# A hybrid layer's kernel: GDN's pools at the right end of memory, attention's first steps beside GDN's last pair, and another tile for two of RWKV's inverses

## The chip, the cores and the metric

The kernel runs on one core of one Trainium2 chip. The metric is the device time of one execution in microseconds (us). TensorE is PE in the rows, its weight loads are PEld, VectorE is DVE, ScalarE is ACT, GpSimd is POOL and SyncE, which here issues DMAs, is SP.

## The reference, cut to what matters

All is float32; 1024 positions (T) of width 1024. Two layers of `first_block` are followed by one `second_block`, which the change doesn't touch.

```python
for layer in range(2):
    h = rms_norm(x, norm_g[layer])
    cols = split_columns(h @ w_in[layer])       # 27 tiles of 128 columns
    y_gdn  = gdn_branch(cols, ...)              # 6 heads, conv of 5, chunks of 64, both directions
    y_mla  = mla_branch(cols, positions, ...)   # 6 heads of softmax attention over 1024 keys
    y_rwkv = rwkv7_branch(cols, ...)            # 4 heads, both directions
    mix = concatenate([y_gdn, y_mla, y_rwkv]) * silu(cols['gate'])
    x = x + mix @ w_out[layer]

# gdn_branch, in a chunk and then over the chunks:
sol = triangular_solve(a_mat, rhs, unit_diagonal=True)      # needs the inverse of a 64x64 triangle
u = u0_c - w_c @ s;  o = qg_c @ s + p_c @ u;  s = ge_c * s + kd_c.T @ u
# mla_branch:
q = rms_norm(cq) @ w_uq;  k, v = rms_norm(ckv) @ w_ukv;  rope on 32 of 96 columns
o = softmax(q @ k.T * scale) @ v
# rwkv7_branch: a token shift, decays and keys, then a scan of the same kind as GDN's
```

The three branches need only `cols`. GDN and RWKV each have a serial scan over chunks; attention has none.

## The kernel before, in words

`layer` (L1658 on) computes one of the two layers in two phases and then the out-projection.

**Phase 1** is the projection beside GDN. The normalised input lies split in two parts, `hh` and `hl`, in pool h. `dense_steps` yields the 1296 products of the 27 tiles one at a time (48 each, `product` L1045, into `psd`), with weights loaded by SP into `wr` and split by ACT and POOL into `wh` and `wl`; ACT evicts `psd` into `st` and sends it to `proj` in DRAM. `paced` ties the products to a count that SP waits on, so that the loads keep step. GDN has three pairs of heads. `gdn_front` is a generator of five stages for one pair: convolution, products, the inverse of the lanes on DVE (`lane_inverse` with `lan`), then on PE L358 to L371 (the inverse's larger blocks), L382, L395 and L405. `gdn_scan` walks over the chunks: L440 writes `psk`, DVE L442 subtracts it, and the output products L428 and L430 go to `pso`; after the last step the norm of the outputs ends with DVE L458.

The string `SEQ_A` is the order of phase 1 as the program is written: a digit is the next stage of that pair, `T6` is six tiles of the projection, `S1` is the scan of pair 1. What is left of the projection, six tiles, is written after `S2`. The scheduler takes this order as priority, not as the final one: it moves an instruction ahead where a tile is free, and the final order of each engine is fixed when the kernel is built.

**Phase 2** is RWKV with attention as its filler. `SEQ_B` lists RWKV's parts: F features, V values, E early, L late, S scan, O output, for the two head groups and the two directions (0 and 1 are one group, 2 and 3 the other; odd ones are the backward direction, `d` = 1). `weave` takes eight steps of `mla` for each round of RWKV's parts, so that attention's 1146 steps are spread over them. `mla` begins with loads by POOL (`mc`, `cq`, `ckv`, L864 to L867), the norms of `cq` and `ckv` (ACT L879, PE L882, ACT L135 and L136), queries (PE L947, L948), rope (DVE and POOL L847 to L850), scores (L974), softmax (L975, L979), the transposes of the probabilities (PE L927 into `ps` of the PSUM pool mT, ACT `ph` L929, DVE `pl` L930) and values (L937 into `pso`).

`rwkv_early` (E) ends with `lan` (DVE L635) and `lane_inverse` on POOL: ACT L468 copies `lan` into `xl`, then 60 POOL instructions (L475, L476) make the inverse in place. `rwkv_late` (L) reads `xl` on DVE (L690) and PE (L698, L705). `lan`, `xl` and `lt` have one buffer each. So the copy for E1 waits until L0 has read `xl`, and that for E3 until L2 has.

Memory: phase 1 opens PSUM as pss 1 bank (the scan's own), pso 1, ps 3, psd 2, and pools h, w, g in SBUF one behind the other from the left. Phase 2 opens after all of these are closed: mT 2 banks, mS 2, rx 3, mo 1, and pools r and s (RWKV) and m (attention), again from the left. So r lies where h was, and RWKV's loads wait until the projection has read h for the last time; m lies further right, where GDN's tiles were.

Of the kernel before, what the change touches and what calls it, by code (L numbers as in the profile page):

```python
# [13 lines left out]
F32 = mybir.dt.float32  # L14
F32R = mybir.dt.float32r
I32 = mybir.dt.int32
AF = mybir.ActivationFunctionType
# [8 lines left out]
SEQ_A = "0 T6 0 1 1 T6 1 0 S0 1 1 2 2 2 T5 S1 2 2 S2"  # L26
# [69 lines left out]
class K:  # L96
# [19 lines left out]
    def psum(self, ex, **banks):  # L116

        return [
            ex.enter_context(self.tc.tile_pool(name=self.name(nm), bufs=b, space=PSUM, reuse_waits="tile"))
            for nm, b in banks.items()  # L120
        ]

    def name(self, s):
        self.n += 1
        return f"{s}_{self.n}"

# [284 lines left out]
def gdn_scan(k, hp, F, prm, y_out):  # L411
# [23 lines left out]
    for s in range(1, NST - 1):  # L435
        psk = k.pss.tile([128, 512], F32, tag="sc", name=n("psk"))
# [12 lines left out]
    for x, sl in zip(y, HALVES):  # L449
        sq = F["free"][1][:, sl]  # L450
        nc.scalar.activation(sq, x, AF.Square)
        ps = k.pss.tile([128, 512], F32, tag="sc", name=n("ps"))
# [9 lines left out]
def lane_inverse(k, eng, pool, lan):  # L462
# [3 lines left out]
    xt = pool.tile([128, 32, 32], F32, tag="xl", name=k.name("xl"))  # L466
# [80 lines left out]
def rwkv_early(k, gi, d, F, prm, P, w2a2, E):  # L547
# [91 lines left out]
    E.update(kb=kb, rk=rk, ga=ga, gb=gb, ep=ep, xl=lane_inverse(k, nc.gpsimd, g, lan))  # L639
# [442 lines left out]
def run(steps):  # L1082
    for _ in steps:
        pass
# [579 lines left out]
def layer(k, L, xs, x_in, x_out, prm_d, prm_at, w_in, w_out, wuq, wukv, cs, next_g):  # L1664
# [3 lines left out]
    with ExitStack() as lx:  # L1668
# [11 lines left out]
        with ExitStack() as hx:  # L1680
            k.pss, k.pso, k.ps, k.psd = k.psum(hx, pss=1, pso=1, ps=3, psd=2)
            hp_ = hx.enter_context(tc.tile_pool(name=n("h"), bufs=1, reuse_waits="tile"))
            hh = hp_.tile([128, 8, T], F32R, name=n("hh"))
            hl = hp_.tile([128, 8, T], F32R, name=n("hl"))
            xs.split_norm(pf("ng"), lambda i, sl: (hh[:, i, sl], hl[:, i, sl]))
            xs.close()
            with ExitStack() as gx:
                wpool = gx.enter_context(tc.tile_pool(name=n("w"), bufs=1, reuse_waits="tile"))
                k.wp = Tagged(wpool, dict(wr=2, wh=3, wl=3, st=2))

                def job(i):
                    def evac(hf, sl, ps):
                        st = k.wp.tile([128, 512], F32, tag="st", name=n("st"))[:, : sl.stop - sl.start]
                        nc.scalar.activation(st, ps, AF.Silu if i >= TI["gate"] else AF.Copy)
                        nc.scalar.dma_start(proj[i][:, sl], st)
                    return w_in[i], ((lambda j: hh[:, j]), (lambda j: hl[:, j])), evac

                steps = dense_steps(k, map(job, ORDER), wait=True)
# [156 lines left out]
```

## Time and profile before

| | us |
|---|---|
| three runs, median (lowest to highest) | 3957.01 (3955.95 to 3962.45) |
| the profiled execution, its own time | 3981.41 |
| its span in the trace | 3979.6 |
| PE busy | 3454.4 (87%) |
| DVE busy | 2349.3 (59%) |
| ACT busy | 1780.1 (45%) |
| POOL busy | 1409.3 (35%) |

In the first layer the projection and GDN run from about 40 to 637 us of the span, RWKV and attention from 637 to 1195, the out-projection to about 1310; the second layer is the same some 1280 us later, and the second block runs from about 2570 to the end. Times below are of the first layer. "Granted clock" (PEclk) is the share of full speed that TensorE was given in a stretch.

### The profile page before, as it was taken

To read this page: it belongs to the slowest core of one execution; us is meant where nothing else is said; L and a number is where in the kernel's file an instruction comes from. 1 tells how busy PE (TensorE), PEld (TensorE's weight loads), DVE (VectorE), ACT (ScalarE), POOL (GpSimd) and SP (SyncE) were. 2 spreads that over 40 slices of the span, in tenths; PEclk is the share of its full clock that TensorE was granted. 3 is DMA by queue.
4 is the path that set the end of the run, shared out by engine and by line. 5 is a ranking of instruction groups with operands and counts; after the bars stand their busy time and mean duration, and the time that the engine had idled before them with its cause. 6 is when DMAs were issued, how large, how long until landed. Compare 5 with 4: busy or idle time off the path is not lost. (4 is left out here: it accounts for less than half of the span.)

```text
span 3979.6 us, 72088 instructions
## 1 busy us (share of the span) xinstructions
PE 3454.4 (87%) x30444; PEld 2710.6 (68%) x30444; DVE 2349.3 (59%) x3138; ACT 1780.1 (45%) x2798; POOL 1409.3 (35%) x1389
## 2 busy tenths in 40 slices
PE   5897996797887889899679899779999998999898
PEld 4666673575665666667357576668888877887786
DVE  6675544857653567462575864359998975323223
ACT  5533425454552553343545454344344347555222
POOL 3431311534403343131163440433333545333361
PEclk9998997898998899899779888879999999999899
DMA  3321211000014232121100000411111111111432
GB/s 115 102 67 47 70 55 66 20 7 4 7 53 166 83 98 68 44 84 49 56 19 7 4 7 33 155 65 46 49 54 51 39 56 46 55 56 41 162 110 72
DMA packets 107076, 237.35 MB, mean 60 GB/s; under 512 B 13896, under 2 KB 16328, under 8 KB 106752
## 3 DMA queue, kind: packets, MB, share of 16 engines
q1 hardware_dynamic: 88448, 197.87, 15.3%
q10 hardware_dynamic: 17280, 31.46, 2.1%
q8 instruction: 239, 3.92, 0.4%
q0 software_dynamic: 1024, 3.41, 0.3%
q14 instruction: 85, 0.70, 0.1%
HBM read 164.17 MB, written 62.23 MB: 57 GB/s over the span
## 5 line engine op out<-in xcount | busy, mean ns | idle before, releaser
L1045 PE MATMUL psd<-hh,wh 128*128 128x512 f32 (+2 forms) x2272 | 910.3, 401 | 56.4 <-ACT hh L1002 18.9
L1006 POOL TENSOR_TENSOR wl<-wr,wh 128x512 fp32r<-128x512 f32 x332 | 489.3, 1475 | 1233.2 <-ACT wh L1002 1193.3
L1045 PE MATMUL psd<-hl,wh 128*128 128x512 f32 (+2 forms) x2272 | 864.9, 381 | 26.7 <-DVE hl L1006 21.6
L1045 PE MATMUL psd<-hh,wl 128*128 128x512 f32 (+2 forms) x2272 | 863.8, 380 | 9.3 <-POOL wl L1006 9.3
L1045 PEld LDWEIGHTS psd<-hh,wh 128*128 128x128 f32 x2272 | 441.4, 194 | 148.4 <-ACT hh L1002 22.9
L1045 PEld LDWEIGHTS psd<-hl,wh 128*128 128x128 f32 x2272 | 440.7, 194 | 100.2 <-DVE hl L1006 27.8
L1045 PEld LDWEIGHTS psd<-hh,wl 128*128 128x128 f32 x2272 | 441.3, 194 | 79.9 <-POOL wl L1006 13.1
L1002 ACT ACTIVATE wh<-wr 128x512 fp32r<-128x512 f32 x332 | 208.3, 628 | 574.4 <-PE psd L1045 345.2
L1211 DVE SCALAR_TENSOR_TENSOR co<-pad,cw,co 128x1024 f32<-128x1024 f32 x240 | 368.7, 1536 | 5.8
L929 ACT ACTIVATE ph<-ps 128x512 fp32r<-128x512 f32 x192 | 114.3, 595 | 198.3 <-PE pso L937 191.0
L930 DVE TENSOR_TENSOR pl<-ps,ph 128x512 fp32r<-128x512 f32 x192 | 131.8, 686 | 91.2 <-ACT ph L929 88.5
L975 DVE TENSOR_REDUCE m<-pss 128x1 f32<-128x512 f32 x192 | 130.6, 687 | 80.2 <-PE pss L974 78.6
L1045 PE MATMUL psd<-hi,wh 128*128 128x512 f32 x384 | 149.7, 393 | 11.7 <-ACT wh L1002 11.7
L937 PE MATMUL pso<-pl,v 128*64 128x256 f32 x384 | 111.4, 324 | 51.9 <-DVE pl L930 51.3
L937 PE MATMUL pso<-ph,v 128*128 128x256 f32 x384 | 134.3, 353 | 23.9 <-DVE y L941 17.4
L1045 PE MATMUL psd<-hi,wl 128*128 128x512 f32 x384 | 149.4, 392 | 5.3 <-POOL wl L1006 5.3
L476 POOL TENSOR_TENSOR xl<-xl,lt 64x30 f32<-64x30 f32 (+14 forms) x240 | 146.3, 609 | 18.1
L1045 PE MATMUL psd<-lo,wh 128*128 128x512 f32 x384 | 149.9, 393 | 0.0
L979 ACT ACTIVATE p<-pss,m 128x512 f32<-128x512 f32 x192 | 129.8, 683 | 44.1 <-DVE m L976 38.5
L1045 PE MATMUL psd<-mh,wh 128*128 128x512 f32 x256 | 102.1, 414 | 48.8 <-ACT wh L1002 35.9
L475 POOL TENSOR_TENSOR lt<-lan,xl 64x30 f32<-64x30 f32 (+14 forms) x240 | 134.1, 559 | 17.9
L927 PE MATMUL ps<-cst,p 128*128 128x128 f32 x768 | 137.8, 302 | 1.1 <-ACT p L979 1.1
(486 smaller groups left out, 7415.2 us busy)
## 6 DMA issues: line engine op xcount, KB each, us to landing
wr<-in_w_in SPq DMA_DIRECT2D x252, 256.0 KB, 2.7
proj<-st ACTq DMA_DIRECT2D x108, 256.0 KB, 2.1
pad<-proj SPq DMA_DIRECT2D x32, 512.0 KB, 3.7
wr<-in_w_out SPq DMA_DIRECT2D x48, 256.0 KB, 2.9
y<-yd SPq DMA_DIRECT2D x16, 512.0 KB, 5.4
sg<-proj SPq DMA_DIRECT2D x16, 512.0 KB, 4.4
x<-x SPq DMA_DIRECT2D x16, 512.0 KB, 4.1
eg<-eg SPq DMA_DIRECT2D x24, 256.0 KB, 4.1
```

Of the source, the lines that this page charges most:

```text
L475: eng.tensor_tensor(t, a, b, op=ALU.mult)
L476: eng.tensor_tensor(x[:, j + 1 :, 0:j], x[:, j + 1 :, 0:j], t, op=ALU.subtract)
L927: yield nc.tensor.transpose(ps[:, c : c + 128], p[i][kt // 4][:, (kt % 4) * 128 : (kt % 4) * 128 + 128], k.c("ident"))
L929: nc.scalar.activation(ph, ps, AF.Copy)
L930: nc.vector.tensor_tensor(pl, ps, ph.bitcast(F32), op=ALU.subtract)
L937: yield nc.tensor.matmul(o, lhsT=l, rhs=r[:, c], start=kt + i == 0, stop=kt + i == 8)
L975: nc.vector.reduce_max(m[:, h : h + 1], pss[h], axis=AX.X)
L979: nc.scalar.activation(p[h], pss[h], AF.Exp, bias=m[:, 2:3], scale=SCALE, accum_out=sums[:, t, h : h + 1])
L1002: first = nc.scalar.activation(hi, src, AF.Copy)
L1006: e.tensor_tensor(lo, src, hi.bitcast(F32), op=ALU.subtract)
L1045: yield nc.tensor.matmul(ps, lhsT=w(a)(i), rhs=x[b](i)[:, sl], start=i == 0 and a == b, stop=i == 7 and a == 1)
L1211: eng.scalar_tensor_tensor(out, pad[:, j : j + T], w[:, j : j + 1], out, op0=ALU.mult, op1=ALU.add)
```

## The change

1. **Pools.** GDN's pool g and RWKV's r and s go to the right end of SBUF; h and w, and then m of attention, lie on the left. In PSUM `pss` is gone: `psk` and the scan's norm take one of the three banks that the front also uses (`k.ps`). `psd` lies left, `pso` and `ps` right. When the projection ends, `psd` and pool h/w close and attention's mS (2 banks), mT (1) and mo (1) open in their place, while GDN still runs. The second bank of mT is opened only with phase 2, on the right; `InTurn` then alternates.
2. **Order.** `SEQ_A` has all remaining eleven tiles ahead of `S1`, and `M60`, `M150` and `M250`, 460 steps of attention, around pair 2's last stages and its scan. `attention` is a generator that first runs out the projection, closes its pools, opens attention's and then yields `mla`'s steps. Phase 2 weaves what is left of them.
3. **Inverse.** In `rwkv_early`, for `d` = 1, the inverse goes into a tile of tag `ec` (`xe`) instead of `xl`.

```diff
-SEQ_A = "0 T6 0 1 1 T6 1 0 S0 1 1 2 2 2 T5 S1 2 2 S2"
+SEQ_A = "0 T6 0 1 1 T6 1 0 S0 1 1 2 2 2 T11 S1 M60 2 M150 2 M250 S2"
...
+class InTurn:
+    def __init__(self, *pools):
+        self.pools, self.at = list(pools), 0
+    def tile(self, *a, **kw):
+        self.at += 1
+        return self.pools[self.at % len(self.pools)].tile(*a, **kw)
...
-        psk = k.pss.tile([128, 512], F32, tag="sc", name=n("psk"))
+        psk = k.ps.tile([128, 512], F32, tag="mm", name=n("psk"))
...
-def lane_inverse(k, eng, pool, lan):
+def lane_inverse(k, eng, pool, lan, xt=None):
-    xt = pool.tile([128, 32, 32], F32, tag="xl", name=k.name("xl"))
+    if xt is None:
+        xt = pool.tile([128, 32, 32], F32, tag="xl", name=k.name("xl"))
...
+    xl = None
+    if d:
+        xl = g.tile([128, NST, CH + 1], F32, tag="ec", name=n("xe")).rearrange("p c i -> p (c i)")[:, :1024]
+        xl = xl.rearrange("p (r c) -> p r c", c=32)
...
-            k.pss, k.pso, k.ps, k.psd = k.psum(hx, pss=1, pso=1, ps=3, psd=2)
+        (k.psd,) = k.psum(hx, psd=2)
+        k.pso, k.ps = k.psum(gx, "right", pso=1, ps=3)
...
+        def attention():
+            run(steps)
+            hx.close()
+            mp = mx.enter_context(tc.tile_pool(name=n("m"), bufs=1, reuse_waits="tile"))
+            k.mS, mT, k.mo = k.psum(mx, mS=2, mT=1, mo=1)
+            k.mT = InTurn(mT)
+            yield from mla(k, mp, [proj[0], proj[TI["cq0"]], proj[TI["ckv"]]], pf, wuq, wukv, cs, ys[3:6])
...
+        k.g = Tagged(gx.enter_context(tc.tile_pool(name=n("g"), bufs=1, side="right", reuse_waits="tile")), GDN_BUFS)
...
+            elif x[0] == "M":
+                run(itertools.islice(others, int(x[1:])))
...
-                    run(steps)
+        gx.close()
+        steps = others
...
-            k.mT, k.mS, k.rx, k.mo = k.psum(px, mT=2, mS=2, rx=3, mo=1)
-            rp, r2, mp = (px.enter_context(tc.tile_pool(name=n(x), bufs=1, reuse_waits="tile")) for x in ("r", "s", "m"))
+            mT, k.rx = k.psum(px, "right", mT=1, rx=3)
+            k.mT.pools.append(mT)
+            rp, r2 = (px.enter_context(tc.tile_pool(name=n(x), bufs=1, side="right", reuse_waits="tile")) for x in ("r", "s"))
```

Line numbers of the changed kernel are 12 to 18 higher in these functions (L407 is the old L395, L900 the old L882, L992 the old L974, L1063 the old L1045). In the order of the changed kernel 116 of attention's steps stand ahead of the end of GDN, 372 to 398 ahead of the end of E1 (185 to 207 before), and its last ones stand in L3's first third (in S3 before).

PE in the first layer, the end of pair 2's front and the start of its scan. In the kernel before, the front's products (L395, then 128 of L405) run in one piece:

```order
L382 MATMUL ps_4857<-gk_3685,am_3739 64x64 x16
L382 MATMUL ps_4875<-vt_3691,am_3739 64x64 x16
L395 MATMUL ps_4894<-kd_3664,gk_3684 64x64 x16
L395 MATMUL ps_4895<-vt_3690,kd_3664 64x64 x16
L395 MATMUL ps_4931<-kd_3664,gk_3684 64x64 x16
L395 MATMUL ps_4932<-vt_3690,kd_3664 64x64 x16
```

The same place in the changed kernel (L407 is the old L395; L965 and L966 are the queries, L925 and L976 keys and values, L992 the scores):

```order
L407 MATMUL ps_5995<-vt_3692,kd_3666 64x64 x11
L965 MATMUL ps_5091<-cq_641_5000,wa_5068 96x512
L966 MATMUL ps_5091<-mc_4999,wb_5069 96x512
L925 MATMUL ps_5082<-wk_5070,ckv_5001 128x128 x4
L976 MATMUL ps_5103<-ckv_5001,wk_5070 64x512
L407 MATMUL ps_5995<-vt_3692,kd_3666 64x64 x5
L407 MATMUL ps_6031<-kd_3666,gk_3686 64x64 x7
L976 MATMUL ps_5107<-ckv_5001,wk_5070 64x512
L407 MATMUL ps_6031<-kd_3666,gk_3686 64x64 x9
L407 MATMUL ps_6032<-vt_3692,kd_3666 64x64 x3
L992 MATMUL pss_5112<-kh_5006,qh_5008 128x512
```

Attention's norms, queries and first scores now stand between the last products of pair 2's front, and the projection's last product ahead of them.

POOL in the first layer, the loads of attention. Before, with projection weights (`wl`) still to be split behind them:

```order
L1006 TENSOR_TENSOR wl_5699<-wr_5680,wh_5698 128x512
L864 DMA mc_5891<-cs 64x1024
L865 DMA mc_5891<-proj_178 64x1024
L866 DMA cq_730_5892<-proj_195 128x1024
L867 DMA ckv_5893<-proj_196 128x1024
```

In the changed kernel (`am` is one of GDN's masks, used in pair 2's front):

```order
L1024 TENSOR_TENSOR wl_4662<-wr_4620,wh_4661 128x512
L401 TENSOR_TENSOR am_3740<-cst_58,ex_697 128x512
L882 DMA mc_4999<-cs 64x1024
L883 DMA mc_4999<-proj_178 64x1024
L884 DMA cq_641_5000<-proj_195 128x1024
L885 DMA ckv_5001<-proj_196 128x1024
```

`wl_4662` is the last of the projection, and the first load, `mc`, waits for PE's last projection product, because m lies where h was; before it waited for an instruction of DVE.

ACT in the first layer, E1's copy of `lan` (L468, in the changed kernel L481) against L0's use of `xl` (L701, L708, in the changed kernel L719, L726; `vz` and `kb` are L0's first work, `ph`, `p` and `y` attention's). Before:

```order
L708 ACTIVATE ga_6141<-ps_7090 32x16x32
L940 ACTIVATE y_6008<-pso_6547 64x512
L929 ACTIVATE ph_6932<-ps_6927 128x512
L701 ACTIVATE xl_6324<-ps_7121 32x512
L468 ACTIVATE xl_6707<-lan_6431 64x1024
L708 ACTIVATE ga_6141<-ps_7139 32x16x32
L719 ACTIVATE av_7171<-ps_7170 64x512
```

In the changed kernel:

```order
L690 ACTIVATE vz_7817<-ps_7936 64x512
L694 ACTIVATE kb_7023<-ps_7942 128x512
L481 ACTIVATE xe_7671<-lan_7399 64x1024
L690 ACTIVATE vz_7817<-ps_7961 64x512
L694 ACTIVATE kb_7023<-ps_7967 128x512
L690 ACTIVATE vz_7817<-ps_7986 64x512
L997 ACTIVATE p_6540,sums_6527<-pss_6528,m_6530 128x512
L947 ACTIVATE ph_6456<-ps_6451 128x512
L997 ACTIVATE p_6541,sums_6527<-pss_6529,m_6530 128x512
L694 ACTIVATE kb_7023<-ps_7992 128x512
L719 ACTIVATE xl_7292<-ps_8016 32x512
```

E1's copy now stands ahead of L0's L719, the first that writes into `xl`; before it stood behind both L701.

## Rows read from the trace of the kernel before

**Rows 1.** Windows by stage: stretch, length, busy PE, PEld, DVE, ACT, POOL; clock, DMA.

```profile
357.00:395.00 38.00, 17.63 (x355) 14.68 (x353) 14.43 (x15) 20.11 (x24) 9.19 (x10) 0.67 0.23 67
...
637.00:712.00 75.00, 47.35 (x173) 26.51 (x172) 52.61 (x78) 37.39 (x60) 5.85 (x17) 0.70 0.12 37
712.00:775.00 63.00, 45.91 (x212) 29.79 (x210) 57.04 (x70) 25.65 (x45) 54.24 (x73) 0.78 0.10 28
775.00:951.00 176.00, 163.58 (x1811) 121.53 (x1811) 114.37 (x195) 96.42 (x195) 46.64 (x74) 0.95 0.02 7
951.00:1031.00 80.00, 55.90 (x393) 40.02 (x394) 59.65 (x92) 27.02 (x58) 42.15 (x67) 0.79 0.00 1
1031.00:1190.00 159.00, 148.86 (x1887) 117.55 (x1886) 90.14 (x163) 91.30 (x179) 42.39 (x72) 0.96 0.07 27
```

**Rows 2.** Timeline of PE, idle pieces in GDN: start, duration, work, idle before.

```profile
372.99 2.07 PE L453 MATMUL ps<-gk,cst 128*128 128x512 f32 x2 [11.88 <-ACT gk L451]
...
387.67 1.97 PE L395 MATMUL ps<-kd,gk 64*64 64x64 f32 x32 [4.84 <-ACT vt L374]
...
521.39 0.31 PE L358 MATMUL ps<-lan,am 32*32 32x32 f32 x2 [5.18 <-DVE lan L350]
```

**Rows 3.** Pair 2's end: PE timeline, and instructions of lines L440 and L1045.

```profile
547.87 1.10 PE L395 MATMUL ps<-kd,gk 64*64 64x64 f32 x32
...
555.34 3.90 PE L405 MATMUL ps<-pt,gk 64*64 64x64 f32 x128
...
L440 PE MATMUL psk<-kd,am x112: 218/218/267, 337.3 to 354.9; 64*64 64x64 f32 x112
...
L440 PE MATMUL psk<-kd,am x112: 218/218/267, 559.1 to 588.1; 64*64 64x64 f32 x112
...
L1045 PE MATMUL psd<-hh,wh x66: 389/395/794, 559.9 to 636.3; 128*128 128x512 f32 x66
...
632.32 0.39 PE L1045 MATMUL psd<-hh,wh 128*128 128x512 f32 x1
632.54 0.39 PE L1045 MATMUL psd<-hl,wh 128*128 128x512 f32 x1
```

**Rows 4.** Timelines of POOL, ACT and PE where attention begins.

```profile
611.59 0.56 POOL L866 DMA_DIRECT2D cq<-proj  x1
...
617.31 0.63 ACT L879 ACTIVATE sq<-cq 128x512 f32<-128x512 f32 x1 [4.08 <-DMA cq<-proj]
...
642.88 1.69 PE L947 MATMUL ps<-cq,wa 128*96 128x512 f32 x2 [3.81 <-ACT sq L135]
...
655.82 0.79 PE L974 MATMUL pss<-kh,qh 128*128 128x512 f32 x1 [2.21 <-ACT qh L1002]
```

**Rows 5.** Timelines of DVE and SP: GDN's last output, RWKV's first load and shift.

```profile
608.55 0.75 DVE L458 SCALAR_TENSOR_TENSOR gk<-gk,prm,gk 128x512 f32<-128x512 f32 x1 [4.44 <-ACT gk L457]
...
637.69 0.42 SPq L495 DMA_DIRECT2D pad<-proj  x1
...
653.65 0.74 DVE L485 TENSOR_SCALAR wa<-pad,rwc 128x1024 f32<-128x1024 f32 x1
```

**Rows 6.** Timelines of DVE and ACT: lanes of E1 and E3 and their copies.

```profile
775.11 3.98 DVE L635 STREAM_TRANSPOSE lan<-ga 32x1024 f32<-32x1024 f32 x2
...
793.57 1.06 ACT L468 ACTIVATE xl<-lan 64x1024 f32<-64x1024 f32 x1 [1.51 <-PE ps L705]
...
1030.91 4.12 DVE L635 STREAM_TRANSPOSE lan<-ga 32x1024 f32<-32x1024 f32 x2
...
1054.83 1.06 ACT L468 ACTIVATE xl<-lan 64x1024 f32<-64x1024 f32 x1 [1.05 <-PE ps L705]
```

**Rows 7.** Windows of the inverses E0, E1, E3, POOL on tile xl alone; clock, DMA.

```profile
717.00:770.00 53.00, 42.52 (x61) 0.74 0.11 33
795.00:830.00 35.00, 29.92 (x60) 0.88 0.01 1
...
1056.00:1093.00 37.00, 30.64 (x61) 1.00 0.01 2
```

**Rows 8.** Windows of the same stretches, DVE alone.

```profile
717.00:770.00 53.00, 47.16 (x63) 0.74 0.11 33
795.00:830.00 35.00, 14.70 (x26) 0.88 0.01 1
```

**Rows 9.** Line L756 in the second layer: a scan with no attention left.

```profile
L756 PE MATMUL psg<-kb,rk x56: 218/242/268, 2451.4 to 2469.5; 64*64 64x64 f32 x56
```

More of the change, by code (lines that the diff above doesn't have):

```diff
@@ L1679, in layer @@
         eg = dp.tile([12, T], F32, name=n("eg"))
[L1680 to L1684 removed]
+        mx, gx, hx = (lx.enter_context(ExitStack()) for _ in range(3))
+        (k.psd,) = k.psum(hx, psd=2)
+        hp_ = hx.enter_context(tc.tile_pool(name=n("h"), bufs=1, reuse_waits="tile"))
@@ L1685, in layer @@
+        hh = hp_.tile([128, 8, T], F32R, name=n("hh"))
+        hl = hp_.tile([128, 8, T], F32R, name=n("hl"))
+        with ExitStack() as nx:
+            (k.ps,) = k.psum(nx, "right", ps=3)
             xs.split_norm(pf("ng"), lambda i, sl: (hh[:, i, sl], hl[:, i, sl]))
             xs.close()
[L1687 to L1698, printed above, removed]
[L1700 to L1720 removed]
@@ new lines, in layer, with job, evac @@
+        k.pso, k.ps = k.psum(gx, "right", pso=1, ps=3)
+        wpool = hx.enter_context(tc.tile_pool(name=n("w"), bufs=1, reuse_waits="tile"))
+        k.wp = Tagged(wpool, dict(wr=2, wh=3, wl=3, st=2))
+        def job(i):
+            def evac(hf, sl, ps):
+                st = k.wp.tile([128, 512], F32, tag="st", name=n("st"))[:, : sl.stop - sl.start]
+                nc.scalar.activation(st, ps, AF.Silu if i >= TI["gate"] else AF.Copy)
+                nc.scalar.dma_start(proj[i][:, sl], st)
+            return w_in[i], ((lambda j: hh[:, j]), (lambda j: hl[:, j])), evac
@@ new lines, in attention @@
+        def attention():
[5 more added lines that the diff above has]
+            yield from mla(k, mp, [proj[0], proj[TI["cq0"]], proj[TI["ckv"]]], pf, wuq, wukv, cs, ys[3:6])
+        steps = dense_steps(k, map(job, ORDER), wait=True)
+        tiles = lambda n: run(itertools.islice(steps, n * 48))
+        tiles(4)
@@ new lines, in layer @@
+        steps = paced(k, steps)
+        others = attention()
+        k.g = Tagged(gx.enter_context(tc.tile_pool(name=n("g"), bufs=1, side="right", reuse_waits="tile")), GDN_BUFS)
+        decays = []
+        fronts = [gdn_front(k, hp, [proj[1 + 3 * hp + a] for a in range(3)], pf, decays, eg) for hp in range(3)]
+        next(fronts[0])
+        misc, _ = pair_of(k, "misc")
+        nc.sync.dma_start(misc, proj[0])
+        decays.extend(gdn_prep(k, misc, pf, eg))
+        next(fronts[0])
+        F = [None] * 3
@@ L1721, in layer @@
+        for x in SEQ_A.split():
+            if x[0] == "T":
+                tiles(int(x[1:]))
+            elif x[0] == "M":
+                run(itertools.islice(others, int(x[1:])))
+            elif x[0] == "S":
+                gdn_scan(k, int(x[1]), F[int(x[1])], pf, ys[int(x[1])])
+            else:
+                F[int(x)] = next(fronts[int(x)])
+        gx.close()
+        steps = others
         with ExitStack() as px:
-            k.mT, k.mS, k.rx, k.mo = k.psum(px, mT=2, mS=2, rx=3, mo=1)
```

30 lines of the change are left out of this document (5 added, 25 removed).

## The prediction, made before the changed kernel ran

> **What bounds the kernel now.** I read the windows by stage first, to see which engine sets each stretch, then the timelines at the places where one stage hands over to the next. [rows 1] hold the stretches of a layer that the change reaches. In most of phase 1 PE is the bound; its exceptions are the hole from 357 to 395, where it worked 17.6 of 38 us at a granted clock of 0.67, with single waits of 11.88 and 4.84 us for pair 1's front, and one of 5.18 at 521 [rows 2]. From 637 to 775 the bound is DVE (52.6 of 75 and 57.0 of 63 us) with POOL's inverse beside it; from 775 to 951 it is PE (163.6 of 176); from 951 to 1031 it is the chain through E2 and E3 (PE 55.9 of 80 at 0.79); from 1031 to 1190 it is PE again (148.9 of 159) [rows 1]. So moving attention's work helps where it leaves a PE-bound stretch, and costs where it lands on a chain.
>
> Both layers run this; I work out one and double it. The second block is left as it is.
>
> **Phase 1: when does GDN end?** Four steps, each against the times of before.
>
> (a) The projection's last product. When the last of pair 2's front products L395 began (547.87), 198 of 1296 projection products were still to come (66 of each kind, 559.9 to 636.3 [rows 3]). In the changed order all stand ahead of that place. At 0.23 us each (632.32 to 632.54 [rows 3]) that is 45 us more PE work. Against it, the scan S0 now runs with projection products instead of pair 1's front, and about 100 more of them stand where the hole was: the three waits alone are 21.9 us, the whole hole 20.4 of idle [rows 1, 2]. S0 itself gets longer, from 17.6 to some 29 us, the length of S2 with the same six products a step [rows 3]; that is inside the 45. I take 25 us back, between 10 (the idle time only moves elsewhere) and 30. The last product, which has some 3 us of pair 2's front behind it, then comes near 545 + 45 - 25 = 565.
>
> (b) Attention's beginning. Its loads now wait for that product, since m lies where h was. Before, from the issue of cq to the Square were 5.7 us, from there to the first queries 25.6, and on to the first score 12.9, 44 in all [rows 4]. About 60 projection products and three evictions stood inside this, so I take 30 and keep 44 as the upper end. Before, the front ran from there to S2 in 14 us: 2.6 of L382, then 547.87 to 559.1 [rows 3]. Now the norms, queries and first scores stand in PE's order between those products, so S2 waits for the chain: 30 + 4 of L405 behind it, S2 begins at 599, 40 us later than the 559 of before. This is what is paid for starting attention early, and 20 us of it is pure chain.
>
> (c) S2. It took 29 us with six projection products a step [rows 3]; now it has three to five of attention's. A scan without filler took 18.1 [rows 9]. With one bank for the transposed probabilities, ph, pl and the next transposes follow each other singly. I take 26, between 20 and 35. S2 ends near 625.
>
> (d) RWKV's start. Before, the first load went at 637.69, held by the last projection product, and the first shift ran 16 us later at 653.65. Now the loads stand behind S2: 625 + 16 = 641. But on DVE the shift also stands behind GDN's last output, which came 20 us after S2's end (608.55) [rows 5]: 645. Phase 1 gains **9 us**. The bounds of (a) to (c) put it between a gain of 30 and a loss of 25.
>
> The edits of `pss` are counted at nothing: the three banks of `ps` have no other use in S1 and S2 than the front, and no projection product needs them; if a front's eviction holds one, it is in the upper end of (c).
>
> **Phase 2.** I counted the order, with durations of this trace. From S2's end to the finish PE has 61 us less work, since attention is ahead by 165 to 200 steps through the first half. By stretch:
>
> (e) First shift to E0's lanes: DVE has 57 us of work where it had 52, and it is the bound there: **5 us** lost. Up to E1's lanes nothing changes: `lan` has one buffer, and E0's inverse sets that stretch (POOL 54.2 of 63 [rows 1]).
>
> (f) E1's lanes to E2's: PE has 161 instead of 153 us of work and is full there, **9 us** lost. The copy for E1 no longer waits from 779 (775.11 + 3.98) to 793.57 [rows 6], 14.5 us, but PE is full there and L1's products queue behind L0's and the scan; I count it at nothing, up to a gain of 10 if PE's other work can follow. E2's lanes to E3's: 4.6 us more PE work in a stretch that PE doesn't bound, **2 us** lost.
>
> (g) E3's lanes to the finish, 159 us [rows 1]. PE's work falls from 137 to 86 us. E3's copy ran at 1054.83 although its lanes were there at 1035.0 (1030.91 + 4.12): 19.8 us [rows 6] that now go. What is late next is the chain behind the inverse: L3's products, the scan S3 (18.1 us where nothing else ran [rows 9]) and the finish follow each other, and only what PE does beside them can go. Of the 31 us by which PE's work falls further I take 13, between none (the chain holds all) and 28 (nearly all of it counts): **33** us, from 20 to 48, and some 5 less at the lower end if POOL gets slower.
>
> By the windows of POOL on xl, the same 60 inverse instructions take 42.5 us where DVE is busy for 47.2 of 53 us and 29.9 where it is busy for 14.7 of 35 [rows 7, 8]. [...]
>
> Phase 2 gains 33 - 5 - 9 - 2 = **17 us**, between 0 and 45.
>
> **The sum.** 9 + 17 = 26 us a layer, 52 for two. Against the profiled execution: 3981.4 - 52 = 3929. That execution lies 24.4 us above the median of the three runs, so against these 3957.0 - 52 = **3905**.
>
> **The rivals.**
>
> *Attention's start holds GDN (slower).* The mechanism is (b) and (c) at their upper ends. PE takes its instructions in order, so whatever of pair 2 stands behind a norm waits for ACT's tables and squares. If the chain lasts the 44 us of before instead of 30, and S2 35 instead of 26, S2 ends at 648, the first shift comes at 668, 14 us later than before. If the hole gives back only 15 of its 25 us, it is 24. Then with phase 2's 17 the layer loses 7, and with its lower half (10) it loses 14: 3957 + 14 to 28, **3978**. The point from which it decides is the first product of S2: with the 17 us of phase 2 the layer loses when it comes later than 599 + 26 = 625. For it: the 44 us are measured, and nothing but the front's own 11 us fills them. Against: the projection's evictions that lengthened the chain are gone.
>
> *The last part stays a chain.* If the stretch after E3's lanes gives only the 20 us of the wait minus slower POOL work, 15 in all, phase 2 gives nothing, and the layer gains 9: **3939**. For it: in the stretch 951 to 1031, which had little to fill it, PE's granted clock was 0.79 against 0.96 in the last stretch [rows 1], and with attention gone the last stretch becomes like it: its 86 us of PE work would cost 104 at that clock. [...]
>
> *Both ends pay.* If the hole is regained in full (30) and the start chain fits in 24, phase 1 gains 20; with 40 in phase 2 the layer gains 60: 3957 - 120, **3840**. Against: both need every cover to hold.
>
> *The change does little.* It plans 460 attention steps beside pair 2 and the order has only 116 ahead of GDN's end. If phase 1's loss (8 to 17) meets phase 2's gain, the time stays within 0.2%, **3957**.
>
> **How the numbers follow.** The forecast (3880 to 3932) has 0.42, the chain at the end (3932 to 3949) 0.11, both ends (3800 to 3880) 0.14, little (3949 to 3965) 0.11, slower 0.22. A measurement of this kernel can tell about 0.2%, 8 us, from no change. So faster 0.67, same 0.11, slower 0.22. The range runs from 3845, with 0.07 below it, to 3985, with 0.1 above it: 0.83 inside.
>
> **What would show it.** (a): the hole after S0 is gone, and the projection's last product comes at 555 to 580. (b): PE idle for 7 to 20 us in pieces between the front's last products, released by ACT's norm; S2's first product near 599. (c): S2's `psk` from first to last in 26 us. (d): first shift near 645 instead of 653.65. (e, f): E2's lanes some 5 us later behind the first shift, in proportion. (g): the copies for E1 and E3 follow their lanes within 3 us, and from E3's lanes to the finish 126 instead of 159 us. The forecast is wrong if S2 begins after 625, if the shift isn't released by S2's end, or if the last stretch keeps over 145 us.

## The result, and the profile after

| | us |
|---|---|
| changed kernel, median of 4 runs (lowest to highest) | 4025.11 (4014.0 to 4030.31) |
| kernel before beside it, median of 4 runs | 3959.73 (3955.95 to 3971.02) |
| ratio, with its 95% interval | 1.0157 [1.0124, 1.0189] |
| profiled execution of the changed kernel, its span | 4030.31, 4028.5 |

The change makes the kernel 1.6% slower, about 65 us by the medians and 49 by the spans of the two profiled executions (before lay above its median, after on its highest run). The forecast was 52 us faster, and the time lies above the range.

Two lines of the page after: the busy times and the granted clock in 40 slices. TensorE was busy 3454.4 us before and has as many instructions as then.

```profile
PE 3537.9 (88%) x30444; PEld 2758.3 (68%) x30444; DVE 2345.0 (58%) x3138; ACT 1784.9 (44%) x2802; POOL 1411.3 (35%) x1389
...
PEclk9899988799878989999878987879999999999899
```

The window from the start of scan S0 to RWKV's finish in layer 1, of before and then of after (columns as in [rows 1]):

```profile
337.30:1190.60 853.30, 722.76 (x8071) 537.19 (x8066) 496.56 (x799) 407.62 (x713) 266.87 (x367) 0.89 0.11 34
```

```profile
335.50:1234.90 899.40, 777.78 (x8071) 568.14 (x8066) 494.40 (x802) 412.32 (x718) 270.56 (x364) 0.86 0.10 33
```

The same 8071 products take 55 us more busy time, while the stretch grows by 46: TensorE's idle time fell from 131 to 122 us. The granted clock stands at one of two levels in both executions, 1.00 or 0.50 (the projection's 128x512 products follow one another every 0.23 us at 545 of after, every 0.43 us at 569). The sums over all pieces of this window in which it stood at the lower one (their length, then TensorE's busy time in them), of before and then of after:

```profile
sum 180.85, PE 114.55 PEld 78.45 DVE 119.78 ACT 67.31 POOL 60.26; mean PE 6.36 PEld 4.36 DVE 6.65 ACT 3.74 POOL 3.35
```

```profile
sum 249.17, PE 206.42 PEld 144.76 DVE 131.75 ACT 83.89 POOL 70.94; mean PE 8.60 PEld 6.03 DVE 5.49 ACT 3.50 POOL 2.96
```

TensorE was busy for 92 us more at the lower level. At half speed that is an estimated 46 of the 55 us. By this count the loss is not more waiting in sum; it is work that runs at the lower clock more often. Why the clock fell more often is another question, and the waits of the new order may be part of the answer. Where it fell is read stage by stage.

**GDN's front.** Windows of after (the projection's last part, in it the place of the old hole, attention's start, scan S2, RWKV's start) and, in the second fence, of before up to L395:

```profile
340.00:587.00 247.00, 226.23 (x2609) 168.00 (x2610) 101.29 (x163) 105.67 (x144) 62.60 (x51) 0.92 0.21 66
...
357.00:395.00 38.00, 34.55 (x668) 27.64 (x669) 16.22 (x18) 24.86 (x34) 11.43 (x11) 0.96 0.34 101
...
587.00:642.00 55.00, 41.85 (x605) 27.22 (x607) 23.45 (x38) 31.49 (x45) 14.57 (x16) 0.84 0.13 42
642.00:670.00 28.00, 26.62 (x359) 19.23 (x355) 16.63 (x39) 11.34 (x26) 1.28 (x1) 1.00 0.01 2
670.00:755.00 85.00, 68.28 (x351) 43.28 (x348) 62.78 (x99) 46.50 (x83) 5.33 (x17) 0.76 0.12 40
```

```profile
340.00:548.00 208.00, 174.34 (x2536) 134.99 (x2538) 101.58 (x163) 92.41 (x128) 56.58 (x47) 0.92 0.21 63
```

**Attention's start**, timeline of after on PE, POOL and ACT: start, duration, work, idle before and what ended it.

```profile
586.55 0.40 PE L1063 MATMUL psd<-hh,wl 128*128 128x512 f32 x1
...
587.26 0.69 POOL L882 DMA_DIRECT2D mc<-cs  x1 [1.66 <-PE psd L1063]
...
596.38 0.63 ACT L897 ACTIVATE sq<-cq 128x512 f32<-128x512 f32 x1 [4.57 <-DMA cq<-proj]
597.06 2.07 PE L900 MATMUL ps<-sq,cst 128*128 128x512 f32 x2 [4.37 <-ACT sq L897]
611.07 2.07 PE L901 MATMUL ps<-sq,cst 64*128 64x512 f32 x2 [4.04 <-ACT sq L898]
628.63 1.94 PE L976 MATMUL ps<-ckv,wk 128*64 128x512 f32 x2 [3.73 <-DVE rt L866]
631.98 0.79 PE L992 MATMUL pss<-kh,qh 128*128 128x512 f32 x1
```

The last projection product ends near 587, the loads go at once, and the first score follows 45 us later. Scan S2 begins only behind the first scores (instructions of L452, the old L440, in its window):

```profile
L452 PE MATMUL psk<-kd,am x112: 218/218/267, 641.9 to 670.0; 64*64 64x64 f32 x112
```

Before it began at 559.1 [rows 3]. GDN's last output, RWKV's first load and shift, and the lanes and copies of E1 and E3, timelines of after on DVE, SP and ACT, against [rows 5, 6]:

```profile
687.98 0.75 DVE L470 SCALAR_TENSOR_TENSOR gk<-gk,prm,gk 128x512 f32<-128x512 f32 x1 [1.34 <-ACT gk L469]
689.23 0.38 SPq L508 DMA_DIRECT2D pad<-proj  x1
693.90 0.74 DVE L498 TENSOR_SCALAR wa<-pad,rwc 128x1024 f32<-128x1024 f32 x1
...
824.53 4.02 DVE L648 STREAM_TRANSPOSE lan<-ga 32x1024 f32<-32x1024 f32 x2
831.82 1.05 ACT L481 ACTIVATE xe<-lan 64x1024 f32<-64x1024 f32 x1
...
1092.90 3.94 DVE L648 STREAM_TRANSPOSE lan<-ga 32x1024 f32<-32x1024 f32 x2
1096.92 1.06 ACT L481 ACTIVATE xe<-lan 64x1024 f32<-64x1024 f32 x1 [1.05 <-DVE lan L648]
```

**The end of the layer**, timeline of PE: the last statistics of RWKV's finish and the first product of the out-projection, after and then before.

```profile
1234.42 1.98 PE L539 MATMUL ps<-sq,cst 128*128 128x512 f32 x4 [1.71 <-ACT sq L820]
1235.84 0.80 PE L1063 MATMUL psd<-mh,wh 128*128 128x512 f32 x1
```

```profile
1190.41 1.99 PE L526 MATMUL ps<-sq,cst 128*128 128x512 f32 x4 [0.58 <-ACT sq L802]
1209.32 0.80 PE L1045 MATMUL psd<-mh,wh 128*128 128x512 f32 x1 [16.92 <-ACT wh L1002]
```

So layer 1 is 40.2 us late at the first shift (693.90 against 653.65), 44.0 at the finish, and 26.5 at the out-projection, which no longer waits 16.92 us for its split weights. Layer 2 repeats it (its out-projection begins at 2549.4 instead of 2501.5), and 49 us remain at the end.

**The clock**, windows of after and then of before:

```profile
552.00:573.00 21.00, 20.53 (x177) 13.51 (x178) 0.59 (x1) 5.87 (x9) 1.28 (x1) 0.51 0.07 27
...
784.00:822.00 38.00, 32.92 (x102) 20.92 (x103) 25.04 (x39) 7.93 (x13) 28.70 (x42) 0.51 0.05 14
...
1166.00:1204.00 38.00, 33.03 (x495) 30.23 (x497) 4.65 (x13) 9.26 (x16) 0.00 (x0) 0.51 0.01 2
```

```profile
537.00:548.00 11.00, 11.00 (x333) 10.17 (x334) 0.00 (x0) 5.77 (x10) 4.40 (x4) 1.00 0.10 27
744.00:782.00 38.00, 29.91 (x174) 20.96 (x173) 36.26 (x48) 17.91 (x31) 26.30 (x39) 0.89 0.10 31
1105.00:1146.00 41.00, 40.20 (x646) 33.13 (x647) 21.36 (x43) 24.75 (x51) 1.33 (x2) 1.00 0.01 2
```

Three stretches of 97 us run at the lower level with TensorE busy for 86 of them; the places of before that correspond to the first and the last (the end of pair 2's front, and L3's products) ran at full clock, the one to the middle (counted from the first shift) at 0.89. In the middle one DVE and POOL do E0's and E1's own work, 25.0 and 28.7 us, so it is not the clock alone that sets it. In the last one, the tail without attention, no other engine is busy for more than 9.3 of 38 us.

### The profile page after: what moved, and what is told of

Read it like the earlier page. It is cut to its first block, busy times and chain, and to the rows that moved or that the text cites. A ratio compares the mean times of both kernels' runs of the same rounds, so it can differ in the third digit from the quotient of the medians.

```text
span 4028.5 us, 72083 instructions
## 1 busy us (share of the span) xinstructions
PE 3537.9 (88%) x30444; PEld 2758.3 (68%) x30444; DVE 2345.0 (58%) x3138; ACT 1784.9 (44%) x2802; POOL 1411.3 (35%) x1389
## 5 line engine op out<-in xcount | busy, mean ns | idle before, releaser
L1063 PE MATMUL psd<-hh,wh 128*128 128x512 f32 (+2 forms) x2272 | 917.3, 404 | 54.3 <-ACT pad L1452 19.5
L1063 PE MATMUL psd<-hl,wh 128*128 128x512 f32 (+2 forms) x2272 | 867.9, 382 | 24.5 <-DVE hl L1024 20.1
L1063 PE MATMUL psd<-hh,wl 128*128 128x512 f32 (+2 forms) x2272 | 867.1, 382 | 14.3 <-POOL wl L1024 14.2
L1063 PEld LDWEIGHTS psd<-hh,wh 128*128 128x128 f32 x2272 | 443.0, 195 | 145.4 <-ACT hh L1020 22.8
L1063 PEld LDWEIGHTS psd<-hl,wh 128*128 128x128 f32 x2272 | 442.7, 195 | 94.4 <-DVE hl L1024 25.7
L1063 PEld LDWEIGHTS psd<-hh,wl 128*128 128x128 f32 x2272 | 443.4, 195 | 85.7 <-POOL wl L1024 19.5
L867 POOL TENSOR_TENSOR rt<-rt,mc 32x512 f32<-32x512 f32 x28 | 37.2, 1330 | 426.9 <-DVE rt L865 404.0
L1063 PE MATMUL psd<-hi,wh 128*128 128x512 f32 x384 | 149.7, 393 | 11.7 <-ACT wh L1020 11.7
L955 PE MATMUL pso<-ph,v 128*128 128x256 f32 x384 | 132.7, 348 | 29.9 <-ACT ph L947 16.5
L1063 PE MATMUL psd<-hi,wl 128*128 128x512 f32 x384 | 149.6, 392 | 5.3 <-POOL wl L1024 5.3
L1063 PE MATMUL psd<-lo,wh 128*128 128x512 f32 x384 | 150.0, 393 | 0.0
L1714 ACT ACTIVATE st<-psd 128x512 f32<-128x512 f32 x108 | 64.2, 594 | 161.7 <-PE psd L1063 160.9
L955 PEld LDWEIGHTS pso<-ph,v 128*128 128x128 f32 x384 | 81.0, 211 | 64.6 <-ACT ph L947 31.2
```

The source lines that it names most:

```text
L867: nc.gpsimd.tensor_tensor(t[96:128], t[96:128], cs[96:128, sl], op=ALU.mult)
L955: yield nc.tensor.matmul(o, lhsT=l, rhs=r[:, c], start=kt + i == 0, stop=kt + i == 8)
L1063: yield nc.tensor.matmul(ps, lhsT=w(a)(i), rhs=x[b](i)[:, sl], start=i == 0 and a == b, stop=i == 7 and a == 1)
```

## The experiments

All times are medians against the kernel before on the same chip; a ratio stands with its 95% interval. Places are of one profiled execution of each kernel, in layer 1 where no other is named.

**The inverse's place alone** (`inv_only`), on the kernel before.

```diff
-    E.update(..., xl=lane_inverse(k, nc.gpsimd, g, lan))
+    xl = None
+    if d:
+        xl = g.tile([128, NST, CH + 1], F32, tag="ec", name=n("xe")).rearrange(...)[:, :1024]
+        ...
+    E.update(..., xl=lane_inverse(k, nc.gpsimd, g, lan, xl))
```

> The kernel before with the third part of the change alone: for d = 1 the inverse goes into a tile of tag ec. Theory A (the early start of attention is what costs, the inverse's own place is worth its wait): the copies for E1 and E3 follow their lanes at once instead of 14.5 and 19.8 us later, E3's lanes to the finish shrink by about 18 us a layer, and the time falls by 20 to 40 us, to 3920 to 3940. Theory B (the inverse's place is worth nothing, since PE is full up to the finish and only the filler moves): within 8 us of before. Theory C (inverses beside busier DVE get slower and hold POOL's other work): slower by 10 us or more.

3964.95 us, 1.0011 [0.9994, 1.0027]: no change. The wait that I priced at 20 us is gone, since E3's copy runs at 1023.51 behind lanes of 1018.51 to 1022.6, yet 164.0 us pass from E3's lanes to the finish, against 159.5 before. The window of `inv_only` over E3's inverse says why, and one row of POOL in it:

```profile
1024.00:1070.00 46.00, 45.47 (x633) 35.41 (x633) 25.35 (x45) 30.88 (x63) 35.14 (x64) 1.00 0.04 14
...
1064.71 1.26 POOL L855 TENSOR_TENSOR rt<-rt,mc 32x512 f32<-32x512 f32 x1 [4.53 <-DVE rt L853]
```

TensorE is full through the whole inverse, as it was beside the wait of before (busy for 18.4 of the 19.8 us), so the wait cost nothing. And the inverse, started earlier, lasts longer for another reason: attention's rope stands among its steps in POOL's order, and it takes 46 us instead of 37 though its own instructions are busy for 30.8 us, as before [rows 7].

**The pools alone, in the old order** (`pools_only`, old inverse), and **pools with the inverse's place** (`pools_inv`), each as a diff against the changed kernel; the first has both edits, the second the first only.

```diff
-SEQ_A = "0 T6 0 1 1 T6 1 0 S0 1 1 2 2 2 T11 S1 M60 2 M150 2 M250 S2"
+SEQ_A = "0 T6 0 1 1 T6 1 0 S0 1 1 2 2 2 T5 S1 2 2 S2 T6 M1"
...
-    if d:
+    if False:
```

> Pools and PSUM as in the change, but the program order of before (five tiles, S1, the rest of the front, S2, then the last six tiles, then attention) and the old place of the inverse. Theory A: the pools cost nothing (psk in the banks of the front, one bank of mT until phase 2), and the out-projection starts some 17 us earlier behind RWKV's finish in each layer, because its pool lies where attention's was: 3925 to 3955. Theory D (the banks are what costs: psk waits for the front's evictions, or the transposes for their single bank): S1 or S2 takes 10 us longer than 55 and 29, and the time is 3980 or more.

> Pools and the inverse's place as in the change, with the program order of before; what is left out against the changed kernel is only the early start of attention. Theory A: the two gains add, 3895 to 3930, so that the early start alone costs 100 us or more against the changed kernel's 4025. If the early start isn't the cause, it stays above 3990.

`pools_only` 3951.25 us, 0.9974 [0.9958, 0.9990], the fastest version of the study that computes the same: 0.26% below before. `pools_inv` 3974.27 us, 1.0023 [1.0006, 1.0040]. So with the new pools and the old order the inverse's own tile costs about 23 us (19 by the ratios), and the early start of attention costs the other 51 (4025 against 3974; 53 by the ratios). The two don't simply add: with the old inverse the early start costs 93 (`after_noxe` below, 4044, against 3951). `pools_only` lies in the range of its Theory A; `pools_inv` misses its 3895 to 3930, so there was no second gain to add. In `pools_only` RWKV's shift comes at 628.6, 25 us earlier than before, but attention's start lies beside it, in this window:

```profile
613.00:666.00 53.00, 28.23 (x48) 9.45 (x48) 30.49 (x39) 39.12 (x48) 6.23 (x15) 0.63 0.18 59
```

and E0's lanes come at 709.1, only 3 us earlier than before. What is kept is the out-projection's start, 1197.6 instead of 1209.3. In `pools_inv` E3's inverse waits in POOL's order for rope again (timeline of POOL):

```profile
1085.48 1.27 POOL L867 TENSOR_TENSOR rt<-rt,mc 32x512 f32<-32x512 f32 x1 [8.06 <-DVE rt L865]
```

From E3's lanes to the finish, windows of `pools_only` and then of `pools_inv`:

```profile
1030.90:1190.10 159.20, 150.19 (x1889) 117.50 (x1887) 90.88 (x163) 94.47 (x181) 42.27 (x69) 0.95 0.05 17
```

```profile
1034.40:1205.40 171.00, 157.72 (x1889) 124.16 (x1887) 93.47 (x166) 93.29 (x182) 42.73 (x69) 0.89 0.08 27
```

The same 1889 products take 12 us longer there, most of it busy time at a lower mean clock. That is where layer 1 loses what the tile costs; why the clock fell there is not shown.

**Attention's start beside the scan instead of pair 2's last stages** (`att_beside_scan`).

```diff
-SEQ_A = "... T11 S1 M60 2 M150 2 M250 S2"
+SEQ_A = "... T11 S1 2 2 M250 S2"
```

> The changed kernel with attention's steps only behind pair 2's front (T11 S1 2 2 M250 S2): norms, queries and first scores no longer stand between the front's last products. Theory A1 (the chain of norms inside the front is the main cost): the first psk of pair 2 comes near 605 instead of 642, though S2 now holds the norms and takes 35 to 50 us; time 3965 to 4000. Theory A2 (it is the projection's last products ahead of the front that cost, and the chain costs the same wherever it stands): S2 ends near 670 as in the changed kernel and the time is 4010 to 4035.

4038.18 us, 1.0203 [1.0183, 1.0223], no better than the changed kernel. In its profiled execution the scan begins 31 us earlier, at 611.0, but takes 41 us instead of 28, so that S2 ends 18 us earlier, the shift comes 11 us earlier (682.6) and the finish 9 (1225.3); by the medians nothing of that is left. S2 moved as Theory A1 said, and yet the time lies above both ranges. The start chain lengthens the scan where it stands beside it, and an earlier end of S2 did not lower the time.

**The norms left out**, in the changed order (`after_nonorm`) and in the old one (`pools_inv_nonorm`).

```diff
-    for sl in HALVES:
-        ...
-        nc.vector.scalar_tensor_tensor(cq0[:, sl], cq0[:, sl], prm("qng")[:, 0:1], s0, ...)
-        ...
-        nc.vector.scalar_tensor_tensor(ckv[:, sl], ckv[:, sl], prm("kvng"), s0, ...)
```

> The changed kernel without the norms of cq and ckv at attention's start (Squares, six sums on PE, Ln and Exp with their table loads, and the scaling are left out, so queries and keys are those of un-normalised inputs). In the changed kernel the projection's last product is at 587, the first score at 632 and the first psk of pair 2 at 642. Theory S (attention's start chain stands in series with GDN there): without norms the chain is loads, queries, rope and scores, some 22 us instead of 45, psk begins near 618 to 622, RWKV's first shift moves by the same, and the time falls by 35 to 55 us to 3970 to 3990. Theory P (the projection's products ahead of the front are what is late): psk moves by under 8 us and the time stays above 4005.

> The kernel with the change's pools and inverse but the order of before, again without the norms of cq and ckv. Here attention's start stands beside RWKV's start, behind GDN. Theory S: the norms lie in parallel there, so that leaving them out gives less than half of what it gives in the changed kernel: 5 to 20 us, 3955 to 3970. If the norms cost the same at either place, the place isn't what matters: 35 us or more, under 3940.

Both kernels leave out the norms, so they compute something else. 4017.06 us, 1.0143 [1.0107, 1.0180], 8 less than with them; and 3922.87 us, 0.9905 [0.9867, 0.9943], 51 less than with them. The chain of norms is cheap in GDN's front, where S2 comes 13 us earlier without it (628.5), and dear beside RWKV's start, where E0's lanes come 20 us earlier without it (688.2). My pricing of the norms as what holds GDN is refuted: without them the changed order is nearly as slow, and it is now 94 us behind the old one.

**The changed kernel with the old inverse** (`after_noxe`).

```diff
-    if d:
+    if False:
```

> The changed kernel with the inverses of d = 1 back in xl; the rest as changed. In the order of before the inverse's own place cost 23 us (pools_inv 3974 against pools_only 3951). If that comes from attention's rope instructions that wait among the inverse's on POOL, it costs in the changed kernel too, where a rope copy held E3's inverse for 9.5 us: 4000 to 4015. If the last part is now bound by the inverse's chain (attention is over by then), the place is worth its wait: 4035 to 4065. Neither: within 8 us of 4025.

4044.22 us, 1.0195 [1.0150, 1.0240]. The interval overlaps that of the changed kernel; in layer 1 E3's copy comes at 1120.2, 13 us behind its lanes, and the finish at 1247.2 instead of 1234.4, of which 4 us were lost before the first shift (697.9). The median lies in the range of the inverse's chain as the bound, but the interval also allows no difference. In this order the tile may be worth something; in the old one it was worth nothing or less. Why the sign differs is open.

**The scan's own bank back** (`pools_pss`), on `pools_only`.

```diff
-        k.pso, k.ps = k.psum(gx, "right", pso=1, ps=3)
+        k.pso, k.ps, k.pss = k.psum(gx, "right", pso=1, ps=3, pss=1)
...
-        psk = k.ps.tile([128, 512], F32, tag="mm", name=n("psk"))
+        psk = k.pss.tile([128, 512], F32, tag="sc", name=n("psk"))
```

> The kernel with the change's pools alone (old order, old inverse), but the scan's own bank pss back, opened beside pso and ps. Theory Q (psk in the front's banks is what moves S1 63 us later and fills the hole at 357 to 395 with projection products): with the bank back S1 begins near 408, the hole is back, pair 2's scan begins near 559 instead of 572, and 117 fewer projection products stand ahead of it; the time is 3950 to 3965, so that the hole's filling was worth 0 to 14 us. If the bank is no part of it, S1 stays near 471 and the time at 3951.

3983.57 us, 1.0045 [1.0020, 1.0071], 32 more than `pools_only` (28 by the ratios). Theory Q is right on the places: S1 begins at 404.5, pair 2's scan at 555.4, and the hole of [rows 2] is back at 362 to 376, at a clock of 0.51. Its price was too low. RWKV's first shift comes 19 us and E0's lanes 34 us earlier than in `pools_only` (674.9), and the finish only 5 us earlier (1185.0); in layer 2 it comes 29 us later. Attention's first score comes 18 us later (684.4 against 666.2). So being early at RWKV's start gave almost nothing by the finish.

**Useless products in the tail**: 128x128 products on constants beside RWKV's last part, at four, two and one of eight steps. `after_fill` also has them in the last output part, the other two don't.

```diff
+            def filler():
+                while True:
+                    for i in range(8):
+                        if i < 4:
+                            ...
+                            nc.tensor.matmul(warm[0][:, :128], lhsT=k.c("ones"), rhs=k.c("ident"), start=True, stop=True)
+                        yield
...
-                weave([...], steps)
+                weave([...], itertools.chain(steps, filler()) if x in ("S2+L32", "O0", "S3", "O1") else steps)
```

> The changed kernel with some 150 useless 128x128 products a layer (ones by identity, into a score bank that attention no longer needs) woven into RWKV's parts from S2+L3 on; nothing of the result changes. In the changed kernel attention is over there, and from 1166 to 1204 TensorE ran at half clock though it was busy 33 of 38 us. Theory K (the last part is lost to the clock): with the added products the granted clock of that stretch is above 0.9, and E3's lanes to the finish take 122 to 134 instead of 142 us although PE has some 17 us more to do; the time falls by 15 to 40 us, to 3985 to 4010. Theory L (the last part is a chain, or PE-bound, at any clock): the stretch keeps its clock or its length, 142 to 160 us, and the time is 4020 to 4060.

> The changed kernel with a quarter as many useless 128x128 fp32 products beside RWKV's last lanes and scan (one step in eight instead of four). In the run with four in eight the added products took 288 records, 37.5 us busy by the row (about 0.13 us each behind one another), the half-clock stretch 1166 to 1204 us was gone, and lanes to finish grew from 142 to 154 us. Theory K (the half clock in the tail costs 33 us of busy TensorE at half rate, so about 16 us a layer): a quarter of the products costs about 9 us; if the clock stays full, lanes to finish is about 142 + 9 - 16 = 135 us and the kernel is about 14 us faster than the changed kernel: 4011 us, ratio 1.013. Rival M (in the tail the chain of steps, not the engine's rate, sets the end): the full clock gives nothing back, lanes to finish is 142 to 151 us, 4025 to 4040 us, ratio 1.016 to 1.020. If the clock does not rise with so few products, the run says only that.

> The same with two steps in eight. Theory K: products cost about 18 us a layer, the full clock gives 16 back: lanes to finish about 144 us, 4029 us, ratio 1.017. Rival M: 152 to 160 us, 4045 to 4060 us, ratio 1.021 to 1.025.

The first is 4064.45 us, 1.0255 [1.0225, 1.0285]; the quarter 4044.07, 1.0205 [1.0187, 1.0222]; the half 4049.13, 1.0230 [1.0210, 1.0251]. None beats the changed kernel, and Theory K's times were missed by all three; in the quarter the clock didn't rise. But they price the clock. Windows of the tail of `after_fill`, and the added products there; then of the quarter:

```profile
1166.00:1204.00 38.00, 36.59 (x644) 34.16 (x643) 3.17 (x8) 10.43 (x18) 0.00 (x0) 0.95 0.01 2
...
L1792 PE MATMUL warm<-cst 128*128 128x128 f32 x288 | 37.5, 280 | 0.0
```

```profile
1167.00:1205.00 38.00, 33.50 (x506) 30.71 (x508) 4.66 (x13) 8.78 (x16) 0.00 (x0) 0.51 0.01 2
...
L1792 PE MATMUL warm<-cst 128*128 128x128 f32 x70 | 9.7, 282 | 0.0
```

| E3's lanes to the last statistics, layer 1 | length | lower clock in it | added products, busy | the other products, busy |
|---|---|---|---|---|
| changed kernel | 141.5 | 64.9 | 0 | 119.2 |
| one in eight | 144.9 | 61.4 | 9.7 | 119.6 |
| two in eight | 150.8 | 54.6 | 18.7 | 118.7 |
| four in eight | 153.8 | 23.9 | 37.5 | 107.3 |

With one and two in eight the clock hardly changed, and the other 1621 products took as long as ever; the stretch grew by less than was added (3.4 and 9.3 us) because some of the added products fell into idle time or ran beside others. With four in eight the lower clock lost 41 us, and the others took 12 us less. The stretch grew by 12.3 us for 37.5 added, so that 25 were given back in all. So in this tail the lower clock cost layer 1 some 12 us by the others' busy time, and at most 19 by what four in eight gave back beyond the 6 of one in eight, whose clock hardly changed (more products may also fall into more idle time). A filler that lifts the clock costs more than that. Layer 2 is no second measurement, since with four in eight 70 more of attention's products fall into its stretch.

## Why the prediction was wrong, step by step

**(a) The projection's last product**, forecast 565 (555 to 580): 587. The 45 us of added products were right in kind (52 measured: 226.2 - 174.3). The step that failed is the 25 us taken back: idle fell from 33.7 to 20.8 us, 13. The hole itself did close (34.6 us busy from 357 to 395 against 17.6 in [rows 1]), but idle came back at other places, 4.6 us up to 433 and 3.1 up to 552; and from 552 to 573 the clock was at its lower level with TensorE busy for 20.5 of 21 us, so that an estimated 10 us of it are due to the clock, more than the 7 us beyond the 45. Even the lower bound of 10 would have given 580.

**(b) Attention's start**, forecast 30 us to the first score and S2 at 599: 45 and 641.9. This was the mis-sized term on which the sum's sign hung. I discounted the measured 44 us [rows 4] for the projection's products inside it (48 by the trace, not about 60); no row showed that they had lengthened it, and with GDN's few products between it takes as long (43.5 us from the issue of cq to the first score). It is a chain of DMA, squares, eight table loads of 1.28 us and rope through ACT and DVE, at a clock of 0.84. PE held the front's products behind it: L407 stopped at 592.7 after 22 of one tile's 32 products, the norm's first sum (L900) waited 4.37 us for ACT's square, and the other ten followed from 599.1. From (a) S2 comes 22 us late, from (b) 21: 15 for the chain and 6 because 10 us instead of 4 pass from the first score to the scan. The upper end of 44 was in the text, and it was the right value for the chain. But `after_nonorm` shows that the norms alone are not the price: without them S2 still begins at 628.5. And these are the places at which the steps came, not shares of the 65 us: where S2 ended earlier (18 us in `att_beside_scan`, 15 in `after_nonorm`), the time fell by 8 us at most.

**(c)** S2 took 28 us, forecast 26. **(d)** The shift came 24 us behind S2's end, forecast 20. GDN's last output released it, though by another way than DVE's order alone: the output ended at 688.7, RWKV's first load went at 689.2, and the shift followed 4.7 us later. Together with (a) and (b): 693.9 instead of 645.

**(e, f)** Shift to E0's lanes took 61.6 us against 58.6 (3 lost, forecast 5), E0 to E1 6 us more (forecast 0), E1 to E2 7.6 more (forecast 9), E2 to E3 5 more (forecast 2). E1's copy ran 7 us behind the start of its lanes instead of 18 (3 behind their end instead of 14.5). Near enough, 21.6 against 16. That E1's copy was worth nothing agrees with `inv_only`, where it is early too and E1's lanes to E2's take 173 us against 176.

**The bank of `pss`**, counted at nothing. `pools_pss` shows that it isn't nothing in the old order: with the own bank back S1 begins 67 us earlier, pair 2's scan 17 us earlier, and the kernel is 32 us slower. So this term was on the change's side, and its size in the new order wasn't measured.

**(g) The last part**, forecast 33 us less: 18. Windows from E3's lanes to the finish, of before and then of after:

```profile
1030.90:1190.40 159.50, 148.96 (x1888) 117.65 (x1886) 90.62 (x163) 91.76 (x179) 42.49 (x72) 0.96 0.08 28
```

```profile
1092.90:1234.40 141.50, 119.18 (x1621) 98.91 (x1621) 50.66 (x93) 61.22 (x113) 34.71 (x65) 0.77 0.08 29
```

Two terms failed. The inverse's wait of 20 us was worth nothing, as `inv_only` shows by itself: TensorE was full beside it (busy for 45.5 of 46 us), and a wait on an engine off the bound should have been priced at nothing. POOL kept its order at both places: in `inv_only` the inverse's step before the rope ended at 1060.2, and its next one ran at 1066.05, directly behind the rope that had waited 4.53 us. In the changed kernel it is a copy of attention's that waited (timeline of POOL):

```profile
1131.28 0.37 POOL L488 TENSOR_TENSOR lt<-lan,xe 64x108 f32<-64x108 f32 x1
1141.15 0.61 POOL L1008 COPY rr<-rs 128x512 f32<-128x512 f32 x1 [9.49 <-PE ps L945]
1141.71 0.38 POOL L489 TENSOR_TENSOR xe<-xe,lt 64x108 f32<-64x108 f32 x1
```

The inverse's last steps stand behind that copy, which waits 9.49 us: L489 runs at 1141.71, although the `lt` that it reads was written by 1131.65. No run shows the 5 us for slower POOL work that stand at the lower end of (g) and in the rival "the last part stays a chain": E3's inverse was busy for 29.9 us in the changed kernel, beside a DVE busy for 18.6 of 47, against 30.6 before [rows 7]. The other term is TensorE's work, which I let fall from 137 to 86 us, by 51. It fell from 149.0 to 119.2, by 30, since 54 us of what was left ran at the lower level, and 12 of the 30 went into idle time. The clock is what the same rival had, at 0.79 for this stretch and with a chance of 0.11; 0.77 was measured.

**The rivals.** "Attention's start holds GDN" is what happened: S2 at 641.9, past its point of decision of 625. Its 3978 was too low: it kept phase 2's gain of 10 to 17, and phase 2 lost 4 (537 us from shift to finish before, 541 after). Without the 17.5 us gained at the out-projection, which the prediction didn't have, it would have been some 35 us worse still; that part of the result is luck.

**What is shown and what stays open.** Shown: the early start is what makes the kernel slower, by 51 us with the inverse's own tile and by 93 without it, and the tile is not the gain; in layer 1 TensorE does the same products with 92 us more of busy time at the lower clock and no more idle time in sum; in the tail that clock costs 12 to 19 us in layer 1. Not shown: why the clock falls more often in the new order, how much of the loss in 552 to 573 and 784 to 822 is cause and how much is only a chain that would wait anyway, how much of the 51 us each of the late steps (a) to (d) costs, and why the inverse's tile lowers the clock in the last part with the pools and costs nothing without them.

## What to carry to other kernels

Price a wait by what the bound engine does beside it: if that engine is full, as here, expect nothing from removing the wait. A filler that is moved forward is taken from behind, so cost both the chain that its start puts in front (at its measured length, without a discount) and the clock of the stretch that it leaves. Compare busy time for equal instruction counts before and after: when busy time grows and idle doesn't, look at the granted clock before you look for a new wait.

## What the runs showed of the hardware

The clock fell in a stretch in which TensorE had not paused for a microsecond since 1157. Timeline of PE in the changed kernel where the lower clock sets in, at 1166, with the last longer wait ahead of it:

```profile
1153.34 0.48 PE L955 MATMUL pso<-pl,v 128*64 128x256 f32 x1 [3.93 <-DVE pl L948]
...
1161.89 1.19 PE L716 MATMUL ps<-xe,ga 32*32 32x32 f32 x32 [0.28 <-ACT vz L690]
1163.76 1.10 PE L723 MATMUL ps<-ga,xe 32*32 32x32 f32 x29 [0.68 <-ACT xe L719]
...
1166.54 1.69 PE L723 MATMUL ps<-ga,xe 32*32 32x32 f32 x31 [0.68 <-ACT xe L719]
```

Around the wait of 3.93 us the clock stood at the lower level from 1153.2 to 1156.6 and then rose. Behind that TensorE ran at full clock, at the end products of 32x32 tiles with waits of 0.28 to 0.68 us; at 1166.8 the clock fell again, and 31 such products take 1.69 us where 29 took 1.10. It stayed low for 37.6 us, in which TensorE was busy for 33.1. Since 1157 no wait had been longer than 0.68 us, while at 552 one of 3.08 us stands just ahead of the fall:

```profile
552.47 0.26 PE L378 MATMUL ps<-am,lan 32*32 32x32 f32 x1 [3.08 <-ACT lan L373]
```

There too TensorE had work: the lower level lasted 20.5 us with TensorE busy for 20.4 of them. With 128x128 products of no use between them (`after_fill`) the 32x32 products of L716 and L723 kept the full clock (32 of them took 1.19 us), and so they did in the kernel before (its L698 and L705, from 1105, 32 in 1.19 us), where attention's products stood between them. But in `pools_inv`, where attention's products stand between them in the same way and TensorE was busy for all of the 17 us ahead, the clock fell behind the last of them; its windows up to and from that place:

```profile
1105.00:1122.00 17.00, 17.00 (x212) 13.42 (x210) 8.10 (x16) 12.61 (x26) 1.90 (x1) 1.00 0.01 2
1122.00:1132.00 10.00, 10.00 (x45) 5.96 (x41) 3.47 (x8) 3.77 (x9) 1.27 (x1) 0.50 0.00 0
```

So neither an idle gap nor the lack of larger products between accounts for this fall. Which property of the stretch lets the clock fall (the small tiles, the short waits, what stood before) is not shown, since no run changed one of them alone.
